# Recurrent scan of a two-layer token mixer: diagonal inverses per segment of four chunks, and log_dt by one contiguous load

## The chip, the cores and the metric

The kernel runs on one core of a Trainium2 chip, in one launch. The metric is the device time of an execution in microseconds (us). A core has five engines that run on their own and meet at semaphores: PE (TensorE, matrix products; its loading of weights is shown as PEld), DVE (VectorE), ACT (ScalarE), POOL (GpSimd) and SP (SyncE, which here only issues DMAs). DMAs are issued by SP, by ACT and by POOL, and sixteen DMA engines carry them out.

## The reference

All data are float32. An input x of 1024 tokens by 1024 features goes through three layers of a network: a gated linear recurrence with a feed-forward part, the "rwkv7" time mix with a feed-forward part, and a hybrid block of a convolution and a diagonal state space (S5). What the change touches lies in two places. The first is the scan of the time mix, for each of 16 heads of 64 features with a state S of 64 x 64:

```
def step(S, inp):
    r_t, w_t, k_t, v_t, a_t, b_t = inp
    sa = einsum('bhvk,bhk->bhv', S, a_t)
    S = S * w_t[:, :, None, :] + sa[..., None] * b_t[:, :, None, :] + v_t[..., None] * k_t[:, :, None, :]
    y = einsum('bhvk,bhk->bhv', S, r_t)
    return S, y
```

The second is the preparation of the S5 part, where each of 32 groups has one value log_dt, and exp(log_dt) multiplies the group's 64 complex rates:

```
dt = exp(log_dt)[:, None]
mag = exp(lr * dt);  ar = mag * cos(li * dt);  ai = mag * sin(li * dt)
```

## The kernel before, in words

Activations lie with the features on the partitions, in tiles of 128 features. The stage that matters here is the time mix. It is one interleaved stage (`weave_`): its parts are written as generators that yield a step (engine, estimated time, what it waits for, what it signals) before the instructions of that step, and a rough clock of the engines decides in which order the steps are issued. The order in each engine's queue is therefore fixed when the program is built, and on the chip each engine works through its queue in that order. The parts are these.

`rwkv_dense` makes the operands of the scan for four segments of 256 tokens. Its `main` runs the projections (L249 to L251 for operands split into a high and a low part, L885 for unsplit ones), `mixes` makes the mixed operands (tiles M and N, `NMP` slots, one mix of 128 features to a slot), `finish` and `stores` put the scan's operands into DRAM, per segment and pair of heads (the last store of a segment is L1038). A mix's slot is free again when the last projection unit that uses it has read it.

`rwkv_scan` works in chunks of 64 tokens, 16 of them, four to a segment, all 16 heads together; two heads (a pair) lie on the partitions. Inside a chunk the recurrence is written with matrices: with A_ab the strictly triangular products of a and b inside the chunk, u = (I - A_ab)^-1 R. For each chunk c:
- `load_bk` loads k and b for half of the pairs (L1114, one slot, `NBK`), `load_q` loads the queries (L1224, slots QT), and `inner` makes the products on PE (L1100) and masks them on DVE into the slot AM of the chunk (L1104). QT and AM have `NAM` slots, so chunk c waits until both halves of chunk c - NAM have been read (signal "y").
- `diagonal` writes the two 32 x 32 diagonal blocks per head of A_ab to DRAM (abD, L1124, four DMAs), and `blocks` loads them back with one block to a partition, four times over: 32 blocks on four groups of 32 partitions (GB, L1133, four DMAs).
- `inverse` starts from rows of the identity (tile `eye`, copied by POOL, L1140) and substitutes: 31 steps s of a product (L1146) and a sum (L1149) on DVE, each over `s // 4 + 1` rows of `31 - s` elements, since each of the four groups of partitions makes every fourth row. Slots GB and YB alternate between two chunks; the last two chunks have slots of their own.
- `inverted` writes the result to DRAM (yiD, L1157, four DMAs that interleave the rows), `whole` loads it into the chunk's matrix YF (L1168, four DMAs), transposes (L1173, DVE) and makes the block below the diagonal with two rounds of small matmuls (L1179, L1189) and ACT copies.
- `turned` brings b, k and v to the tokens' side (L1202 to L1219), `chain` carries the state from chunk to chunk, for two halves of the pairs: R (L1244, L1247, L1250), u (L1255, L1258), then the new state (L1264, L1270, L1274). `outs` makes y (L1289, L1291, L1293), `post` norms and gates it (L1303 to L1324).

`rwkv_out` adds the output projection (mm<-XO, L249 to L251, and HO, L1419) for the first 768 tokens, as soon as the last segment is stored and chunks 7 and 11 are done. After the stage the feed-forward part begins with a norm (sums L273, spread L281, tile ms).

`s5_prep` prepares the S5 part. Its instructions are spread over the feed-forward part that follows, but its first DMAs wait for nothing there: POOL issues them as soon as it has come to them. They are the rates (L1475 to L1477) and log_dt, once as a whole to all partitions (L1479), and twice with every second group, to 64 partitions each (L1481), for 16 columns that hold groups in pairs.

Of the kernel before, what the change touches and what calls it, by code (L numbers as in the profile page):

```python
# [14 lines left out]
P = 128  # L15
# [10 lines left out]
NAM = 3  # L26
# [11 lines left out]
NMP = 13  # L38
# [18 lines left out]
class Net:  # L57
    """Feature-major activations: tile [128 features, 512 tokens] per (k, half)."""
# [15 lines left out]

    def open_group(self, T, W, S, L, psum):
        """Pools of one part of the net: T and S slots of [128, 516], weight slots, PSUM banks per tag."""
        self.close_group()
        self.bigx = ExitStack()
        self.nT = T
        self.big = self.bigx.enter_context(self.tc.tile_pool(name="big", bufs=1, reuse_waits="tile"))  # L80
        self.open_work(W, S, L, psum)

    def open_work(self, W, S, L, psum):
        """All of them but T anew."""
# [8 lines left out]
    def open_top(self):  # L93
        """One more pool above the group's, closed before them."""
        self.close_top()
        self.topx = ExitStack()
        self.top = self.topx.enter_context(self.tc.tile_pool(name="top", bufs=1, reuse_waits="tile"))

    def open_rtop(self):
        """Another one, from the other end of the memory."""  # L100
# [44 lines left out]
    def s(self, dt=F32, n=HT):  # L145
        """scratch [128, n <= 516]"""
# [3 lines left out]
    def extra(self, tag, shape, dt, every, bufs):  # L150
        """now and then a slot of the pool on the right, where that is for more of the others"""
# [7 lines left out]
    def ld(self, src=None, n=HT, rows=P):  # L159
        """tile for a load; loads have slots of their own, for they run ahead"""  # L160
# [66 lines left out]
    def load_ws(self, srcs, nk, m, tag="w"):  # L227
        """srcs: DRAM APs arranged [p, nk, n] for columns c..c+n; returns hi, lo tiles [P, nk, m]"""
# [17 lines left out]
    def mm3(self, ps, w, x, first, last):  # L246
        """ps += w.T @ x with w = (hi, lo), x = (hi, lo)"""
# [5 lines left out]
    # W columns [c0, c0+128) for all nk row tiles  # L253
# [3 lines left out]
    def lin(self, w, xs, nk):  # L257
        """xs: list of (hi, lo) per k -> PSUM tile"""
# [6 lines left out]
    def rstd_bcast(self, acc, scale, eps, acc2=None):  # L265
        """acc [128, 512] -> PSUM [128, 512]: (sum over partitions * scale + eps)^-0.5 on all partitions; with acc2,
        for which that is the factor of another norm: that one and the product of both"""
# [34 lines left out]
    def square(self, h, k, half, gain=None):  # L302
        """h[k][half] is final: its part of the sum of squares (and of that of the products with the gain)"""
# [60 lines left out]
    def blocks(self, nblk, units, in_unit, post, nk_out, wout, h, add_bias=None, lag=2, delay=3, mid=None, late=None, fill=None, nlate=LATE):  # L364
        """units: weight items per block; in_unit(b, i, half, w) ; post(b, half) -> list of nk_out (hi, lo)"""
# [51 lines left out]
        # the first half of the last block before the second half of the one before it  # L417
# [34 lines left out]
    def hawk(self, h, xn, mid, late):  # L452
# [5 lines left out]
        # c8 = 8 softplus(-lam), softplus(z) = max(z, 0) + log1p(exp(-|z|)), log1p(e) = 2 atanh(e / (2 + e))  # L458
# [100 lines left out]
    def ple_prep(self, layer):  # L559
        """p, features on the partitions, split"""  # L560
# [40 lines left out]
    NSEG, SN = 4, 256  # token segments of the dense part  # L601

    def rwkv_consts(self):
# [7 lines left out]
        # block-diagonal ones (2 heads), identity minus the same / 64, and per-head selector columns  # L611
# [8 lines left out]
        # [s, t] masks on both heads: s < t | s <= t  # L620
# [19 lines left out]
        # operands of the scan, one chunk of 64 tokens after another  # L640
        self.qD, self.bkD, self.gbD = (d((16, P, KD, 2, 64), nm) for nm in ("qD", "bkD", "gbD"))
        self.vD = d((16, P, KD, 64), "vD")
        # second factors of the low-rank parts, for one pair after another
# [5 lines left out]
        # per head pair the decays between chunk middles; at the segments' ends in two factors  # L649
# [12 lines left out]
    def rwkv_norm_late(self, hD, rs, half, gain, sig):  # L662
        """A task: the same for the other half, with the factors [tokens, token tiles] known"""
# [22 lines left out]
    def weave_(self, tasks, banks):  # L686
        """Issues the steps of generators in the order in which a rough clock of the engines would start them.
        tasks: (generator, head start in us or a function of PE time and own PE time). banks: PSUM banks per tag.
        A generator yields step(...) before the instructions of that step."""
        clk = {e: 0.0 for e in "PAVGSQD"}  # Q: descriptors, D: transfers  # L690
        free = {tag: [(0.0, f"{tag}{i}") for i in range(n)] for tag, n in banks.items()}
        held, done = {}, {}
        # PE's clock halves after a window of little work, until one of much; windows of several phases
# [70 lines left out]
    def step(eng, us, lat=None, wait=(), sig=(), bank=None, rel=None, par=False, dma=None, use=1.0):  # L764
        """eng: PE, Act, Vector, GpSimd, SP (then us: transfers, lat: their time); us: time on it; lat: after it; wait,
        sig: what it waits for and what is done with it; bank: PSUM tag to take a bank of; rel: bank to give back;
        par: the next step doesn't wait for this one; dma: transfers it starts and their time; use: share of PE's rows and columns."""
# [4 lines left out]
    # r, k, v, the low-rank parts, and from them the operands of the scan (in DRAM)  # L772
# [1513 lines left out]
```

## Time and profile before

| | us |
|---|---|
| median of three runs | 4200.29 |
| lowest and highest | 4192.26, 4203.89 |
| span of the profiled execution, first to last instruction | 4186.6 |
| PE busy in it | 3949.4 |
| DVE busy in it | 2544.7 |
| ACT busy in it | 1466.1 |
| DMA, mean over the span | 111 GB/s |

The profiled execution's own time is not recorded apart from its span; the median lies 13.7 us above the span. In the rows further down a time is counted from the span's start. "Busy" is the time in which an engine has an instruction in work. A matmul's end is modelled, so a busy PE is not a PE at its peak. The clock that PE was granted (PEclk) has two levels, 1.2 and 2.4 GHz; a row gives its mean as a share of 2.4.

### The profile page before, as it was taken

The numbers are of one execution on the slowest core, as the hardware profiler recorded it, in microseconds if no ns is written. First come the engines' busy times: TensorE is split into PE (matmuls) and PEld (weight loads), VectorE is DVE, ScalarE is ACT, GpSimd is POOL, SyncE is SP. The second block draws the span as 40 slices with busy tenths as digits, with TensorE's granted clock in tenths as the row PEclk, the third lists the DMA queues.
The fourth block names the chain that finished last, engine by engine and source line by source line (L and its number), as shares of the span: only waits on it lengthen the run. The fifth ranks groups of instructions, "written<-read, shape, count | busy, mean of one in ns | idle before, by whom it ended". The sixth has DMA issues, their size and how long they took to land.

```text
span 4186.6 us, 58441 instructions
## 1 busy us (share of the span) xinstructions
PE 3949.4 (94%) x22510; PEld 3216.6 (77%) x22510; DVE 2544.7 (61%) x5192; ACT 1466.1 (35%) x2491; POOL 179.3 (4%) x376
## 2 busy tenths in 40 slices
PE   6998999999988999999999699999999999999899
PEld 5776788888877877777867587888887877888687
DVE  6665733333364678777756476354536599997655
ACT  4455511111132665554542241111113332222533
POOL 0000000000000000000000101010100000000000
PEclk8999999999998999989979799999999999999999
DMA  3111111111122789676776541212211244332775
GB/s 103 48 47 34 51 46 51 41 56 51 34 67 88 216 252 237 174 209 170 194 194 173 97 127 52 63 49 66 63 49 58 71 119 118 109 115 96 236 226 186
DMA packets 695830, 464.49 MB, mean 111 GB/s; under 512 B 197956, under 2 KB 620800, under 8 KB 695552
## 3 DMA queue, kind: packets, MB, share of 16 engines
q1 hardware_dynamic: 514272, 367.80, 30.0%
q10 hardware_dynamic: 175872, 83.90, 7.3%
q0 software_dynamic: 5408, 9.06, 1.1%
q8 instruction: 177, 2.90, 0.3%
q14 instruction: 101, 0.83, 0.1%
HBM read 355.51 MB, written 106.69 MB: 110 GB/s over the span
## 4 chain that ended last, share of the span: by engine, by line
PE 69%; DVE 12%; DMA 7%; ACT 5%; issue 4%; SPq 1%; POOL 1%; ACTq 0%; DVEq 0%; POOLq 0%
PE mm L249 15%; PE mm L251 14%; PE mm L250 14%; PE ob L249 4%; PE ob L250 4%; PE ob L251 4%; DVE cy L1882 3%; PE g L1100 2%; PE g L926 1%; PE g L1438 1%; PE y L1291 1%; DMA BK<-bkD 1%; PE y L1289 1%; DVE w L863 1%; PE mm L2073 1%
## 5 line engine op out<-in xcount | busy, mean ns | idle before, releaser
L249 PE MATMUL mm<-T,w 128*128 128x512 f32 (+1 forms) x2944 | 1152.6, 393 | 47.1 <-ACT w L215 22.5
L251 PE MATMUL mm<-T,w 128*128 128x512 f32 (+1 forms) x2944 | 1149.9, 391 | 9.6 <-DVE w L216 9.6
L250 PE MATMUL mm<-T,w 128*128 128x512 f32 (+1 forms) x2944 | 1150.3, 392 | 1.1 <-DVE T L1380 0.9
L249 PEld LDWEIGHTS mm<-T,w 128*128 128x128 f32 x2944 | 558.6, 190 | 174.3 <-ACT w L215 26.9
L251 PEld LDWEIGHTS mm<-T,w 128*128 128x128 f32 x2944 | 559.0, 190 | 126.8 <-DVE w L216 12.1
L250 PEld LDWEIGHTS mm<-T,w 128*128 128x128 f32 x2944 | 559.7, 190 | 117.5 <-DVE T L1380 1.7
L215 ACT CAST w<-wraw 128x1024 fp32r<-128x1024 f32 (+1 forms) x286 | 288.4, 1014 | 988.8 <-PE mm L250 700.2
L216 DVE TENSOR_TENSOR w<-wraw,w 128x1024 fp32r<-128x1024 f32 (+1 forms) x286 | 335.1, 1177 | 373.9 <-ACT w L215 371.1
L389 DVE TENSOR_TENSOR h<-ob,h 128x512 f32<-128x512 f32 x416 | 286.1, 690 | 230.7 <-PE ob L251 227.5
L249 PE MATMUL ob<-S,w 128*128 128x512 f32 x896 | 359.2, 401 | 21.7 <-DVE h L389 21.1
L1882 DVE SCALAR_TENSOR_TENSOR cy<-cu,pv,cy 128x512 f32<-128x512 f32 x480 | 350.9, 749 | 12.3 <-ACT cy L1880 2.6
L250 PE MATMUL ob<-S,w 128*128 128x512 f32 x896 | 354.7, 396 | 0.2 <-DVE S L216 0.2
L251 PE MATMUL ob<-S,w 128*128 128x512 f32 x896 | 354.7, 396 | 0.0
L249 PE MATMUL mm<-M,w 128*128 128x256 f32 x768 | 255.1, 332 | 16.4 <-ACT M L837 8.5
L250 PE MATMUL mm<-N,w 128*128 128x256 f32 x768 | 229.7, 299 | 4.4 <-DVE N L839 4.3
L251 PE MATMUL mm<-M,w 128*128 128x256 f32 x768 | 229.8, 299 | 4.3 <-DVE w L863 4.0
L249 PEld LDWEIGHTS ob<-S,w 128*128 128x128 f32 x896 | 169.9, 190 | 70.2 <-DVE h L389 30.2
L251 PEld LDWEIGHTS ob<-S,w 128*128 128x128 f32 x896 | 169.7, 189 | 38.6
L250 PEld LDWEIGHTS ob<-S,w 128*128 128x128 f32 x896 | 170.1, 190 | 36.3 <-DVE S L216 0.6
L249 PEld LDWEIGHTS mm<-M,w 128*128 128x128 f32 x768 | 157.0, 204 | 50.3 <-issue 23.3
L439 DVE TENSOR_TENSOR S<-mm,S 128x512 f32<-128x512 f32 x88 | 60.8, 690 | 211.7 <-PE mm L251 209.8
L215 ACT CAST S<-S 128x512 fp32r<-128x512 f32 x128 | 79.3, 620 | 266.3 <-DVE S L439 154.4
(458 smaller groups left out, 5431.9 us busy)
## 6 DMA issues: line engine op xcount, KB each, us to landing
wraw<-in_rw_w_rkv_dram ACTq DMA_DIRECT2D x96, 512.0 KB
wraw<-in_ffn_w_in_dram SPq DMA_DIRECT2D x88, 512.0 KB
wraw<-in_w_in_dram SPq DMA_DIRECT2D x48, 512.0 KB
wraw<-in_ffn_w_out_dram SPq DMA_DIRECT2D x44, 512.0 KB
BK<-bkD SPq DMA_DIRECT2D x64, 256.0 KB
wraw<-in_rw_w_o_dram ACTq DMA_DIRECT2D x24, 512.0 KB
wraw<-in_lru_w_in_dram SPq DMA_DIRECT2D x20, 512.0 KB
wraw<-in_ple_w_gate_dram SPq DMA_DIRECT2D x16, 512.0 KB
```

The lines of the kernel that those rows point to most:

```text
L215: self.nc.scalar.copy(hi, x)
L216: self.nc.vector.tensor_sub(lo, x, hi.bitcast(F32))
L249: nc.tensor.matmul(ps, w[0], x[0], start=first, stop=False)
L250: nc.tensor.matmul(ps, w[0], x[1], start=False, stop=False)
L251: nc.tensor.matmul(ps, w[1], x[0], start=False, stop=last)
L389: nc.vector.tensor_add(h[m][half], ps, h[m][half])
L439: nc.vector.tensor_mul(a, ps, sg.pop((b, j, half)))
L863: nc.vector.tensor_sub(wl.rearrange(fl), r.rearrange(fl), wh.bitcast(F32).rearrange(fl))
L926: nc.tensor.matmul(ps, lw[r0:r1, slot, :], HW[hx][r0:r1], start=x == 0, stop=x == len(rows) - 1)
L1100: nc.tensor.matmul(g[:, 128 * x : 128 * x + 128], bk[rs, x].rearrange("p a b -> p (a b)"), qt[rs, j0 + x].rearrange("p a b -> p (a b)"), s ...
L1289: nc.tensor.matmul(o[rs], s[rs, x], qz[rs, j, 1, :], start=True, stop=False)
L1882: nc.vector.scalar_tensor_tensor(y, x[:, k : k + HT], cw(k), y, ALU.mult, ALU.add)
```

## The change

The inverses of the four chunks of a segment are made together. One block lies on one partition: chunk c takes the 32 partitions from 32 * (c % 4), so four chunks fill 128. A step s then covers `s + 1` rows instead of `s // 4 + 1`, and the 31 steps run once per segment. GB and YB have one slot each for all segments (YB 32 x 32 elements instead of 8 x 32), blocks are loaded once instead of four times, and the result is written by one DMA instead of four. The first step waits for the blocks of all four chunks, the loads of a segment's blocks wait for the substitution of the segment before. POOL sets the identity by two memsets. XT and WL share a tile (XW). NAM goes from 3 to 4 and NMP from 13 to 11. In `s5_prep` the two strided loads of log_dt go; two DVE copies take the pairs' columns from the load that stays. The diff also takes out comments and docstrings, which are not shown.

```diff
-NAM = 3
+NAM = 4
-NMP = 13
+NMP = 11
...
-        G, Y = slots("GB", (P, 32, 32), 2, NG), slots("YB", (P, 8, 32), 2, NG)
+        G, Y = (self.tiny(nm, (P, 32, 32), 1) for nm in ("GB", "YB"))
...
-        eye = self.tiny("eye", (P, 8, 32), 1)
-        nc.gpsimd.memset(eye, 0.0)
-        for e in range(4):
-            r = eye[32 * e : 32 * e + 32]
-            nc.gpsimd.affine_select(out=r, in_=r, compare_op=ALU.not_equal, fill=1.0, base=-e,
-                                    pattern=[[-4, 8], [1, 32]], channel_multiplier=0)
...
         def blocks():
             for c in range(NC):
-                yield E("S", 4, 1.46, wait=[("ab", c)] + ([("sub", c - 2)] if 2 <= c < NG else own(c)), sig=[("in", c)], par=True)
-                src = D.pop(c).rearrange("h x j s t -> (h x j) s t")
-                for e in range(4):
-                    nc.sync.dma_start(G(c)[32 * e : 32 * e + 32], src)
-
-        def inverse(q):
-            for c in range(q, NG, 2) if q < 2 else [q]:
-                yield E("G", 0.97, wait=[("in", c)] + ([("yd", c - 2)] if 2 <= c < NG else own(c)))
-                g, y = G(c), Y(c)
-                nc.gpsimd.tensor_copy(y, eye)
+                yield E("S", 1, 0.73, wait=[("ab", c)] + ([("sub", c // per - 1)] if c >= per else []), sig=[("in", c)], par=True)
+                r0 = 32 * (c % per)
+                nc.sync.dma_start(G[r0 : r0 + 32], D.pop(c).rearrange("h x j s t -> (h x j) s t"))
+
+        def inverse():
+            for seg in range(NC // per):
+                yield E("G", 1.2, wait=[("yd", c) for c in range(per * (seg - 1), per * seg)] if seg else ())
+                nc.gpsimd.memset(Y, 0.0)
+                nc.gpsimd.memset(Y.rearrange("p a b -> p (a b)")[:, 0:1024:33], 1.0)
                 for s in range(31):
-                    nj, n = s // 4 + 1, 31 - s
-                    us = 0.07 + nj * n / 960
-                    yield E("V", us, lat=ILAT)
-                    w = self.tiny(f"TB{q % 4}", (P, 80), 2)[:, 0 : nj * n].rearrange("p (j t) -> p j t", t=n)
-                    nc.vector.tensor_mul(w, y[:, 0:nj, s : s + 1].to_broadcast([P, nj, n]),
-                                         g[:, s : s + 1, s + 1 :].to_broadcast([P, nj, n]))
-                    yield E("V", us, lat=ILAT, sig=[("sub", c)] if s == 30 else ())
-                    nc.vector.tensor_add(y[:, 0:nj, s + 1 :], y[:, 0:nj, s + 1 :], w)
+                    nk, n = s + 1, 31 - s
+                    us = 0.07 + nk * n / 960
+                    yield E("V", us, lat=ILAT, wait=() if s else [("in", c) for c in range(per * seg, per * seg + per)])
+                    w = self.tiny("TB", (P, 256), 1)[:, 0 : nk * n].rearrange("p (j t) -> p j t", t=n)
+                    nc.vector.tensor_mul(w, Y[:, 0:nk, s : s + 1].to_broadcast([P, nk, n]),
+                                         G[:, s : s + 1, s + 1 :].to_broadcast([P, nk, n]))
+                    yield E("V", us, lat=ILAT, sig=[("sub", seg)] if s == 30 else ())
+                    nc.vector.tensor_add(Y[:, 0:nk, s + 1 :], Y[:, 0:nk, s + 1 :], w)
 
         def inverted():
             for c in range(NC):
-                yield E("S", 4, 0.73, wait=[("sub", c)], sig=[("yd", c)], par=True)
-                yD = self.dram.tile([2, 2, 8, 32, 32], F32, name=self.n("yiD"))
-                ye = yD.rearrange("h x j (k e) t -> e (h x j) k t", e=4)
-                for e in range(4):
-                    nc.sync.dma_start(ye[e], Y(c)[32 * e : 32 * e + 32])
-                D[c, 1] = yD
+                yield E("S", 1, 0.73, wait=[("sub", c // per)], sig=[("yd", c)], par=True)
+                r0 = 32 * (c % per)
+                D[c, 1] = yD = self.dram.tile([2, 2, 8, 32, 32], F32, name=self.n("yiD"))
+                nc.sync.dma_start(yD.rearrange("h x j k t -> (h x j) k t"), Y[r0 : r0 + 32])
...
-                XT = self.tiny("XT", (P, 8, 32), 1)
+                W = self.tiny("XW", (P, 256), 1)
+                XT = W.rearrange("p (j t) -> p j t", t=32)
...
-                W = self.tiny("WL", (P, 256), 1)
...
-            yield E("S", 9, 1.22, wait=list(wait))
+            yield E("S", 7, 1.22, wait=list(wait))
...
             dma(dt[:, 0:32], ldt.partition_broadcast(P))
-            for b in range(2):
-                dma(dt[64 * b : 64 * b + 64, 32:48], ldt[b:32:2].partition_broadcast(64))
...
+            yield V(16)
+            nc.vector.tensor_copy(dt[lo, 32:48], dt[lo, 0:32:2])
+            yield V(16)
+            nc.vector.tensor_copy(dt[hi, 32:48], dt[hi, 1:32:2])
```

## Rows read from the trace of the kernel before

**Rows 1.** The page's busy line: busy us (share of the span) xinstructions.
```profile
PE 3949.4 (94%) x22510; PEld 3216.6 (77%) x22510; DVE 2544.7 (61%) x5192; ACT 1466.1 (35%) x2491; POOL 179.3 (4%) x376
```

**Rows 2.** Stretches of the scan's stage: length, busy us (xinstructions) by engine, PEclk, DMA, GB/s.
```profile
core 0: us, PE busy (x) PEld busy (x) DVE busy (x) ACT busy (x) POOL busy (x), PEclk, DMA share, GB/s
1560.00:1960.00 400.00, 384.83 (x3922) 315.92 (x3920) 300.39 (x968) 214.78 (x488) 28.41 (x76) 0.93 0.75 199
1960.00:2168.00 208.00, 199.59 (x2208) 158.36 (x2204) 150.04 (x489) 103.73 (x238) 17.80 (x41) 0.90 0.68 180
2168.00:2340.00 172.00, 159.16 (x1644) 128.73 (x1641) 105.31 (x345) 51.70 (x96) 14.34 (x19) 0.89 0.61 176
2340.00:2394.00 54.00, 19.84 (x201) 14.94 (x200) 8.72 (x19) 9.38 (x21) 3.30 (x5) 0.55 0.55 67
```

**Rows 3.** Timeline near 2340: start, us, engine, line, xcount, [idle before, what ended it].
```profile
2338.20 1.66 POOL L1481 DMA_DIRECT2D pv<-in_ssm_log_dt_dram  x2
2340.65 21.20 SPq L1157 DMA_DIRECT2D yiD<-YB  x4
2366.76 0.44 DVE L1173 STREAM_TRANSPOSE XT<-YF 32x256 f32<-32x256 f32 x1 [14.36 <-DMA YF<-yiD]
2367.25 0.31 PE L1179 MATMUL g<-XT,AM 32*32 32x32 f32 x2 [26.58 <-DVE XT L1173]
```

**Rows 4.** DMA view of 2338 to 2363: a queue's packets and share; issues, landing us.
```profile
q0 software_dynamic: 136, 0.03, 71.3%
pv<-in_ssm_log_dt_dram POOLq DMA_DIRECT2D x2, 4.0 KB, 18.0
```

**Rows 5.** Timeline near 2285, where chunk 14 goes the same way.
```profile
2282.16 2.52 SPq L1157 DMA_DIRECT2D yiD<-YB  x4
2286.18 1.81 SPq L1168 DMA_DIRECT2D YF<-yiD  x4
2289.93 0.90 DVE L1173 STREAM_TRANSPOSE XT<-YF 32x256 f32<-32x256 f32 x2
```

**Rows 6.** A small DVE copy in the S5 preparation: duration in ns, minimum, median, maximum.
```profile
L1486 DVE COPY pv<-ms x1: 198/198/198, 2461.0 to 2461.0; 128x48 f32<-128x48 f32 x1
```

**Rows 7.** Groups from 1100 to 2600 us, DVE: busy us, mean ns, idle before.
```profile
L1146 DVE TENSOR_TENSOR TB<-YB,GB 128x60 f32<-128x60 f32 (+24 forms) x496 | 99.0, 208 | 19.2 <-DMA GB<-abD 9.3 <-POOL YB L1140 1.8 <-DMA L<-rkD 0.4
L1149 DVE TENSOR_TENSOR YB<-YB,TB 128x60 f32<-128x60 f32 (+24 forms) x496 | 98.0, 207 | 7.4
L1013 DVE TENSOR_TENSOR L<-L,F 128x256 f32<-128x256 f32 x32 | 13.3, 417 | 2.8 <-ACT F L1009 2.8
```

**Rows 8.** The same view, PE: first matmuls on split mixed operands.
```profile
L249 PE MATMUL mm<-M,w 128*128 128x256 f32 x768 | 255.1, 332 | 16.4 <-ACT M L837 8.5 <-ACT w L861 7.7
```

**Rows 9.** SP's timeline, 2164 to 2290 us: a store, two loads, a write.
```profile
2165.25 0.37 SPq L1038 DMA_DIRECT2D gbD<-GBs  x1
2187.17 0.32 SPq L1114 DMA_DIRECT2D BK<-bkD  x1
...
2232.73 2.55 SPq L1157 DMA_DIRECT2D yiD<-YB  x4
2235.66 0.33 SPq L1114 DMA_DIRECT2D BK<-bkD  x1
```

**Rows 10.** DVE's timeline: inverse of chunk 12; last mask and inverse of chunk 15.
```profile
2205.83 0.19 DVE L1146 TENSOR_TENSOR TB<-YB,GB 128x31 f32<-128x31 f32 x1 [1.22 <-DMA GB<-abD]
...
2302.94 0.69 DVE L1104 TENSOR_TENSOR AM<-g,msk 128x512 f32<-128x512 f32 x1 [5.76 <-PE g L1100]
...
2312.78 0.18 DVE L1146 TENSOR_TENSOR TB<-YB,GB 128x31 f32<-128x31 f32 x1
```

**Rows 11.** PE's timeline: u of chunks 13, 14 and 15; next stage's spread.
```profile
2284.48 1.98 PE L1255 MATMUL ch<-R,YF 64*64 64x64 f32 x32
...
2308.33 1.15 PE L1255 MATMUL ch<-R,YF 64*64 64x64 f32 x32
...
2372.04 1.97 PE L1255 MATMUL ch<-R,YF 64*64 64x64 f32 x32 [0.88 <-ACT YF L1194]
...
2393.76 0.58 PE L281 MATMUL ms<-ident,rs 128*128 128x128 f32 x1 [1.73 <-POOL rs L290]
```

More of the change, by code (lines that the diff above doesn't have):

```diff
@@ L1119, in diagonal @@
                 yield E("S", 4, 0.73, wait=[("am", c)], sig=[("ab", c)], par=True)
-                abD = self.dram.tile([2, 2, 8, 32, 32], F32, name=self.n("abD"))
+                D[c] = abD = self.dram.tile([2, 2, 8, 32, 32], F32, name=self.n("abD"))
                 for hd in range(2):
@@ L1125, in diagonal @@
                                           AM(c)[r0 : r0 + 32, :, hd, 0, 32 * x : 32 * x + 32])
-                D[c] = abD
         def blocks():
             for c in range(NC):
-                yield E("S", 4, 1.46, wait=[("ab", c)] + ([("sub", c - 2)] if 2 <= c < NG else own(c)), sig=[("in", c)], par=True)
-                src = D.pop(c).rearrange("h x j s t -> (h x j) s t")
-                for e in range(4):
-                    nc.sync.dma_start(G(c)[32 * e : 32 * e + 32], src)
-        def inverse(q):
-            for c in range(q, NG, 2) if q < 2 else [q]:
-                yield E("G", 0.97, wait=[("in", c)] + ([("yd", c - 2)] if 2 <= c < NG else own(c)))
-                g, y = G(c), Y(c)
-                nc.gpsimd.tensor_copy(y, eye)
-                for s in range(31):
-                    nj, n = s // 4 + 1, 31 - s
-                    us = 0.07 + nj * n / 960
-                    yield E("V", us, lat=ILAT)
-                    w = self.tiny(f"TB{q % 4}", (P, 80), 2)[:, 0 : nj * n].rearrange("p (j t) -> p j t", t=n)
-                    nc.vector.tensor_mul(w, y[:, 0:nj, s : s + 1].to_broadcast([P, nj, n]),
-                                         g[:, s : s + 1, s + 1 :].to_broadcast([P, nj, n]))
-                    yield E("V", us, lat=ILAT, sig=[("sub", c)] if s == 30 else ())
-                    nc.vector.tensor_add(y[:, 0:nj, s + 1 :], y[:, 0:nj, s + 1 :], w)
@@ L1330, in outputs @@
                 nc.sync.dma_start(self.outD[:, :, 64 * c : 64 * c + 64].rearrange("j p t -> p j t"), O[c % 2])
-        return ([chain(0), chain(1), outs(0), outs(1), whole(), [inverse(q) for q in [0, 1, *range(NG, NC)]], blocks(), turned(), [inner(), load_bk()], diagonal(),
+        return ([chain(0), chain(1), outs(0), outs(1), whole(), inverse(), blocks(), turned(), [inner(), load_bk()], diagonal(),
                  inverted(), load_q(), post(), outputs()])
```

## The prediction

> **What bounds the kernel now.** I read the page's busy line first [rows 1]: PE is busy 3949.4 of 4186.6 us, DVE 2544.7. As a whole the kernel hangs on PE, so an edit that removes DVE work pays only where PE waits. The profiled execution has a span of 4186.6 us; the median of the three runs is 4200.29, so some 13.7 us lie around the span if that execution was a median one (the fastest, 4192.26, leaves 5.7). I work with differences and put them on the median.
>
> The second view is the table by stretches of the stage that the change touches, the recurrent mixer, from 1560 us, when its scan begins, to 2394 [rows 2]. Up to 2168 us PE is busy about 96% of the time at 0.90 to 0.93 of its clock. Until 2340 us it is still 159.16 of 172. In the last stretch, 54 us long, it works 19.84 us at 0.55 of the clock. So there is slack in one place only: the end of the scan, where chunk 15 (the last of 64 tokens) is finished while nothing else is left.
>
> The third view is the timeline of those 54 us [rows 3]. POOL issues the two strided log_dt loads of the next stage's preparation at 2338.20. SP begins to write chunk 15's inverses (yiD<-YB) at 2340.65, and these four issues take 21.20 us. The transpose of the blocks, loaded back from there, follows at 2366.76, and PE resumes at 2367.25 after 26.58 us idle, the longest gap of the stage. The DMA view of 2338 to 2363 names who was in the way [rows 4]: POOL's queue q0 moved 0.03 MB in 136 packets and held 71.3% of sixteen engines' time; the two log_dt loads, 4 KB each, took 18.0 us in the median to land.
>
> **log_dt.** The change drops both strided loads; the contiguous one was there already. What the write costs without them I take from chunk 14 [rows 5]: issue at 2282.16, all four in 2.52 us, next load at 2286.18, transpose at 2289.93, so 7.77 us from write to transpose. For chunk 15 it is 2366.76 - 2340.65 = 26.11. The term is 26.11 - 7.77 = 18.3 us, taken from the path that sets the end, as PE has no other work there. Bounds: 0 if something else held the write; 18.3, not 26.58, as the normal 7.8 us stay. In return DVE copies 64 x 16 elements twice; a copy of 128 x 48 takes 198 ns [rows 6], so under 0.4 us, on a DVE that was busy 8.72 of 54 us [rows 2]. Uncovered, ACT's exponential comes 0.4 us later.
>
> The Trainium skill (DMA: Bandwidth & Descriptors, "Queues, rings and completion order") says that each DMA engine takes turns between the queue rows that have work, packet by packet. Read as a fair share, SP's writes would have lost only half their rate, the term would be about 9 us and the forecast 4191. The row speaks for nearly the whole.
>
> **The inverse on DVE.** Before, each chunk has 31 steps of a product and a sum, 62 operations x 16 chunks = 992, on average (1560 elements over 31 steps) 50 elements per partition, at 208 and 207 ns [rows 7]: 992 x 0.2075 = 206 us. After, 62 x 4 segments = 248 operations, (s+1)(31-s) elements, 5456 over 31 steps, 176 on average. 256 elements take 417 ns [rows 7]; the line through both is 1.02 ns an element, so 176 take 0.335 us and the sum is 83 us. DVE loses 123 us and 744 instructions, but up to 2168 us that lies beside a PE that is 96% busy [rows 2], and PE's waits for DVE are small. SP issues 10 instead of 16 DMAs a chunk (96 fewer, at 0.63 us as in the write's 2.52 for four [rows 5], 60 us of queue time). I credit both with 8 us of PE waits, between 0 and the 24 us that PE idles from 1560 to 2168 (608 - 584.42) [rows 2]. POOL's two memsets a segment replace four copies and run while the blocks are still on their way; XT and WL become one tile, but WL was written after XT had been read before too; TB's one buffer is written and read on DVE alone: all three nothing, at worst a wait of one operation, 0.3 us.
>
> **Slots.** NAM 3 to 4 gives each chunk of a segment its own products (AM) and queries. It is paid with two of 13 slots for mixed operands (NMP 11). PE's first matmuls on those operands waited 16.4 us in all, 8.5 of it for ACT's cast [rows 8]. With 11 slots five mixes instead of three are made during a last unit; I take 4 us more, between 0 and 20 (as much again, and some). Earlier segments cost nothing else: their scan has the next segment's projections beside it; without that cover each waits one inverse, some 30 us.
>
> **The end of the scan, rebuilt.** Here the change adds a wait: the inverse of chunk 12 now waits for the blocks of chunk 15. Behind it on DVE stand the transposes and state updates of chunks 12 to 15, and for those PE and ACT wait.
> 1. The last segment is stored at 2165.25; the half-chunk loads of the products (BK, one slot) go from 2187.17 to 2235.66 in five steps [rows 9], 9.7 us each. Without the slot wait the eighth goes at 2245.4, and the last mask of chunk 15 comes one step later, 2255, instead of 2302.94 [rows 10], where chunk 15 waited until chunk 12 had given its slot back. The first of these steps also waited for chunk 11's remainder, which will be done earlier: I take 2250 (2232 to 2258).
> 2. Mask to first operation of the inverse: 2302.94 to 2312.78 [rows 10], 9.8 us: 2260.
> 3. The inverse: 62 x 0.335 = 20.8 us plus other DVE work in between. For chunk 12 the wall time was 2205.83 to 2232.73 [rows 9, 10], 26.9 for 12.9 of its own, 14 of other work; I take 10: 2291 (21 to 35 us).
> 4. Write, load, transpose: 7.8 as above: 2299.
> 5. Transpose to u of chunk 12: as for chunk 15, 2366.76 to 2372.04 [rows 3, 11], 5.3: 2304.
> 6. Three more chunks. Bounds: chunk 15 alone kept PE 19.84 us at 0.55 of the clock [rows 2], 11 us at full clock; chunk 13's u to chunk 14's was 23.85 us with projections in between [rows 11]; R2 below has 30. I take 19 each: 2361.
> 7. u of the last chunk to the next stage's first spread (ms): 2372.04 to 2393.76, 21.7 [rows 11], at half the clock; I take 20: 2381.
> Against 2393.76 that is -13. So the tail gains less than the 18.3 of log_dt: the batch itself costs 5 there. With -8 for waits and +4 for slots the sum is -17, rounded to -18: **4182**.
>
> **Rivals.**
> R1, given back: steps 1 and 3 at their late ends (+8, +4) and the slots at +10 turn the sum of -17 into about +1: 4200. For it: PE had only 13 us of gaps from 2168 to 2340 [rows 2], so chunk-by-chunk inverses were well covered. Against it: the slot wait of chunk 15 goes.
> R2, slower: the chain at half clock. The projection matmuls (mm<-XO) that now lie between the chunks can run while the batch waits for its blocks. If they are used up before step 5, PE pauses, its clock falls to 1.2 GHz as in the last 54 us [rows 2], and four chunks of small matmuls run at it: chunk 15's 19.84 us, some 4 more for the update of the state and the turned operands that chunk 15 has behind it or doesn't need, and with gaps 30 instead of 19: +33 in step 6, +2 in step 7, 4217. It decides from the point where those matmuls run out 10 us or more before the first u. For it: chunk 15 alone ran so. Against it: while they last the clock is full, 0.89 on average to 2340.
> The Trainium skill (TensorE: Matmul & The Clock Gate, Part 1) says that PE's clock follows how busy PE has lately been, and that idle time halves it; by that rule every pause that the batch makes costs twice, which is R2's price. The trace agrees at 2340 to 2394.
> R3, more: step 1 at its early end (-18) and step 6 at 14 each (-15), as PE has less beside the chunks than in the 23.85 us; two thirds of both is 22 us, 4160. For it: the slot wait and the POOL and SP work of the last chunk of the third segment are gone. Against it: one BK slot, so the pace of 9.7 us stays.
> R4, the log_dt edit does not do what it says, or by half: if the write was held by turns and not wholly, 9 us come back instead of 18.3, 4191, and if other traffic held it, none, 4200.
>
> **Numbers.** Forecast 4182 (own range 4168 to 4190), chance 0.36. R3 0.14, R1 0.25, R2 0.21, R4 0.04. What a measurement can tell from no change is 0.3%, 12.6 us. Faster by more: 0.33 of the forecast's 0.36 plus R3's 0.14, 0.47. Same: 0.03 + R1's 0.25 + R4's 0.04 less 0.01 at R1's upper end, 0.31. Slower: 0.21 + 0.01, 0.22. The range runs from just below R3 to just above R2, 4150 to 4220.
>
> **What would show it.** No gap of over 12 us on PE in front of the last transposes, and yiD's issue at about 0.6 us: log_dt right. 124 products of the inverse in place of 496, at 0.33 us mean: the inverse right. First operation of the last inverse near 2260 and its last near 2291 after the span's start: steps 1 to 3. The u of chunks 12 to 15 some 19 us apart, at full clock: step 6; some 30 apart at 0.5 of the clock would be R2. Waits of PE for the mixes (L249) far above 20 us would make the slots' term wrong. The forecast falls if chunk 12's u comes after 2325, or if the stage before 2165 moves by more than 10 us.

## The result and the profile after

The change made the kernel slower: 4215.6 us in the median of six runs against 4197.8 us of the kernel before, ratio 1.0054 (95% interval 1.0034 to 1.0074), some 18 to 23 us. The forecast was 4182 us. The profiled execution of after has a span of 4218.3 us and took 4219.97 us, the longest of its six; that of before has 4186.6 us, and since some 2 us lie around the span in other runs of before, it was about 9 us faster than the median. So 14 of the 31.7 us between the two spans are scatter, and sizes are taken below from the timed runs, places from the traces.

The page's busy line after, against [rows 1]: PE works 24 us longer, VectorE 84 us less with 742 instructions fewer (the durations of its instructions, added up, fall by 122; where two overlap, the busy time counts them once).

```profile
PE 3973.7 (94%) x22510; PEld 3228.4 (77%) x22510; DVE 2460.5 (58%) x4450; ACT 1468.5 (35%) x2491; POOL 177.3 (4%) x361
```

At 1340 us the two traces are level within 0.4 us, and of the 32.6 us by which the last matmul is later, 30.9 have arrived at the first spread of the next stage. So the time went in the mixer's stage. In it PE is busy 979.0 us (1340 to 2425) where it was 960.5 (1340 to 2394), for the same 9241 matmuls, and idle 106 us instead of 94. Its stretches after, with the columns of [rows 2]:

```profile
core 0: us, PE busy (x) PEld busy (x) DVE busy (x) ACT busy (x) POOL busy (x), PEclk, DMA share, GB/s
1560.00:1960.00 400.00, 381.73 (x3589) 309.51 (x3585) 266.92 (x612) 216.91 (x491) 30.55 (x72) 0.94 0.70 191
1960.00:2100.00 140.00, 133.94 (x1507) 111.66 (x1503) 87.77 (x191) 69.57 (x150) 8.89 (x22) 0.98 0.67 184
2100.00:2160.00 60.00, 56.26 (x482) 38.74 (x482) 26.19 (x68) 23.93 (x60) 4.13 (x16) 0.50 0.48 120
2160.00:2340.00 180.00, 157.58 (x1478) 126.77 (x1476) 84.39 (x170) 49.88 (x93) 5.88 (x5) 0.84 0.55 164
2340.00:2425.00 85.00, 60.14 (x1013) 48.91 (x1008) 23.04 (x49) 29.57 (x65) 11.56 (x15) 0.81 0.41 118
```

The third row stands out. From 2100 to 2160 us PE runs at half its clock and does 482 matmuls; the same window before, in the first row below, has 601 at 0.84. The last projection starts at 2092 us after and at 2137 before: after, the projections have run ahead of the scan, and what is left is the scan's own matmuls, most of 64 columns, and the last operands of the fourth segment.

```profile
2100.00:2160.00 60.00, 57.19 (x601) 41.56 (x602) 42.00 (x141) 28.84 (x72) 5.79 (x18) 0.84 0.63 159
2140.00:2160.00 20.00, 18.34 (x130) 11.72 (x132) 12.72 (x35) 9.41 (x26) 1.29 (x7) 0.52 0.61 138
2160.00:2180.00 20.00, 17.09 (x169) 12.12 (x166) 6.67 (x16) 6.05 (x13) 0.00 (x0) 0.55 0.84 245
```

But before has such a stretch too, behind its own last projection: the second and third row, which the stretches of [rows 2] hide. And the kernel of experiment 6 below, which is faster than after, has one as early:

```profile
2100.00:2120.00 20.00, 14.96 (x48) 8.17 (x50) 16.18 (x51) 7.80 (x21) 2.20 (x9) 0.50 0.58 142
2120.00:2140.00 20.00, 14.19 (x216) 11.04 (x215) 11.29 (x30) 6.88 (x16) 0.15 (x1) 0.59 0.73 186
```

So the half clock alone does not tell after from before. What does is the time from the last projection to the last store of the segment: 90 us after (2092 to 2181), 28 before (2137 to 2165), 50 in experiment 6 (2083 to 2132). Here the projections' first matmuls on split operands, before and then after, from the view of their tile; the last two times of a row are the first and the last start:

```profile
L249 PE MATMUL mm<-M,w x768: 277/285/687, 1352.3 to 2137.0; 128*128 128x256 f32 x192
L249 PE MATMUL mm<-M,w x768: 276/285/775, 1348.8 to 2091.6; 128*128 128x256 f32 x192
```

The end of the scan after, from the timeline: last store of the last segment, first and last operation of the last inverse, the write, the transposes, u of chunk 12, the last spread.

```profile
2181.39 0.46 SPq L1038 DMA_DIRECT2D gbD<-GBs  x1
...
2282.76 0.19 DVE L1138 TENSOR_TENSOR TB<-YB,GB 128x31 f32<-128x31 f32 x1 [0.82 <-DMA GB<-abD]
...
2315.43 0.22 DVE L1141 TENSOR_TENSOR YB<-YB,TB 128x31 f32<-128x31 f32 x1
...
2319.07 1.87 SPq L1148 DMA_DIRECT2D yiD<-YB  x4
...
2326.34 0.90 DVE L1165 STREAM_TRANSPOSE XW<-YF 32x256 f32<-32x256 f32 x2 [3.93 <-DMA YF<-yiD]
...
2336.25 1.15 PE L1246 MATMUL ch<-R,YF 64*64 64x64 f32 x32
...
2424.66 2.08 PE L281 MATMUL ms<-ident,rs 128*128 128x128 f32 x8 [1.34 <-POOL rs L290]
```

The write takes 1.87 us for four chunks where that of chunk 15 alone took 21.20 [rows 3], and the transpose follows 7.3 us behind it. But the segment is stored 16 us later than before [rows 9] (the third one at 1938 us in both), the u of chunk 12 comes at 2336, and the spread 31 us later than in [rows 11].

### The profile page after: what moved, and what is told of

It is laid out like the page before. It is cut to its first block, busy times and chain, and to the rows that moved or that the text cites. A ratio compares the mean times of both kernels' runs of the same rounds, so it can differ in the third digit from the quotient of the medians.

```text
span 4218.3 us, 57574 instructions
## 1 busy us (share of the span) xinstructions
PE 3973.7 (94%) x22510; PEld 3228.4 (77%) x22510; DVE 2460.5 (58%) x4450; ACT 1468.5 (35%) x2491; POOL 177.3 (4%) x361
## 4 chain that ended last, share of the span: by engine, by line
PE 68%; DVE 13%; DMA 7%; issue 6%; ACT 4%; POOL 1%; SPq 0%; ACTq 0%; DVEq 0%; POOLq 0%
PE mm L249 14%; PE mm L251 14%; PE mm L250 14%; PE ob L249 4%; PE ob L250 4%; PE ob L251 4%; DVE cy L1875 3%; PE g L1094 2%; PE g L926 2%; PE mm L885 1%; DVE w L863 1%; DMA BK<-bkD 1%; DVE w L216 1%; PE g L1429 1%; PE y L1282 1%
## 5 line engine op out<-in xcount | busy, mean ns | idle before, releaser
L249 PE MATMUL mm<-M,w 128*128 128x256 f32 x768 | 252.8, 329 | 18.4 <-ACT M L837 11.1
```

The lines of the kernel that those rows point to most:

```text
L249: nc.tensor.matmul(ps, w[0], x[0], start=first, stop=False)
```

## The experiments

Each was timed against the kernel before; the ratio is to that, with its 95% interval. There were three series (1 to 4, 5 to 8, 9 to 11), in which the kernel before had medians of 4197.1, 4195.7 and 4204.6 us; from one series to another the ratios compare better than the medians.

**1. log_dt alone**

```diff
 (the kernel before)
-            for b in range(2):
-                dma(dt[64 * b : 64 * b + 64, 32:48], ldt[b:32:2].partition_broadcast(64))
...
+            nc.vector.tensor_copy(dt[lo, 32:48], dt[lo, 0:32:2])
+            nc.vector.tensor_copy(dt[hi, 32:48], dt[hi, 1:32:2])
```

> The kernel before with the log_dt edit alone (two strided loads gone, two copies on VectorE in their place); all else as before. My term: the write of chunk 15's inverses is no longer held by POOL's strided loads, write to transpose goes from 26.1 to about 8 us, and 18 us come off the end of the scan: 4180 us against 4198, ratio 0.9956, and the 26.6 us gap on PE becomes about 8. Rival (something else held that write): no change, 4198, with the gap still there. Half (the queues shared the engines): 4189.

Measured: 4175.0 us, 0.9951 (0.9933 to 0.9968), 21 us less. In the timeline the write of chunk 15 goes straight through, its transpose comes 6.6 us later, and PE's gap of 26.58 us [rows 3] is 7.11. The profiled execution is the slowest of the eight, and this write comes 16 us later in it than in [rows 3]:

```profile
2356.55 2.69 SPq L1157 DMA_DIRECT2D yiD<-YB  x4
...
2363.14 0.44 DVE L1173 STREAM_TRANSPOSE XT<-YF 32x256 f32<-32x256 f32 x1 [5.07 <-DMA YF<-yiD]
...
2363.64 0.31 PE L1179 MATMUL g<-XT,AM 32*32 32x32 f32 x2 [7.11 <-DVE XT L1173]
```

**2. The batch with the strided loads put back**

```diff
 (the kernel after)
+            for b in range(2):
+                dma(dt[64 * b : 64 * b + 64, 32:48], ldt[b:32:2].partition_broadcast(64))
-            nc.vector.tensor_copy(dt[lo, 32:48], dt[lo, 0:32:2])
-            nc.vector.tensor_copy(dt[hi, 32:48], dt[hi, 1:32:2])
```

> The kernel after with the two strided log_dt loads of before put back: the batched inverse alone. In the trace of after POOL issues its contiguous log_dt load at 2392.2 us, just ahead of the store of chunk 14's outputs (2397.7 us), and chunk 15's group norm waits for that store. If strided loads hold whatever SP writes next for some 18 us, that store lands about 15 to 18 us later and the kernel takes 4231 to 4234 us. Rival (nothing on the path is issued behind them now, or the loads' price was peculiar to the write of the inverses): 4216, as after.

Measured: 4234.5 us, 1.0102 (1.0074 to 1.0129), 19 to 20 us above after. So log_dt is worth the same in both kernels, though here it holds up other work. ACT's exponential, which stands in front of chunk 15's squares, waits for the loads, and the store of chunk 14, for which the squares wait too, lands 21 us after its issue instead of 4. The squares start at 2420.11 instead of 2402.08, in an execution that was 1.9 us behind by then:

```profile
2417.78 0.24 ACT L1480 ACTIVATE pv<-pv 128x48 f32<-128x48 f32 x1 [19.91 <-DMA pv<-in_ssm_log_dt_dram]
2420.11 0.60 ACT L1297 ACTIVATE psq<-g 128x512 f32<-128x512 f32 x1 [2.09 <-DMA outD<-psq]
```

**3. Eleven slots alone**

```diff
 (the kernel of experiment 1)
-NMP = 13
+NMP = 11
```

> The kernel before with the log_dt edit and 11 instead of 13 slots for mixed operands (NMP); the inverse still chunk by chunk, three slots of products. Theory S, the slots: in the trace of after the last segment is stored 16.5 us later than before (2181.9 against 2165.3), and two slots fewer alone do that; then this kernel takes about 16 us more than the log_dt edit alone, near 4196 us. Theory B, the batch: the scan falls behind because four chunks wait for one inverse; then this kernel is within 4 us of the log_dt edit alone, near 4180 us, and its last store stays near 2165.

Measured: 4238.8 us, 1.0109 (1.0087 to 1.0132): 64 us above the log_dt edit alone, four times what theory S said. The whole stage, first with 13 slots (experiment 1), then with 11:

```profile
1340.00:2389.00 1049.00, 963.11 (x9243) 788.57 (x9244) 712.41 (x2120) 524.92 (x1155) 73.11 (x176) 0.90 0.71 192
```

```profile
1340.00:2436.00 1096.00, 987.57 (x9234) 802.69 (x9235) 713.83 (x2119) 526.93 (x1154) 78.85 (x176) 0.88 0.68 183
```

That is 47 of the 64 us, in the slowest execution of the one kernel and one of the faster of the other. The same matmuls take 24 us more at a lower clock, and PE idles 108 us instead of 86. The projections come later (below in the same view, first with 13 slots, then with 11: the last starts at 2185 instead of 2149) and part of the scan earlier: the u of chunk 7, the last of the second segment, starts at 1930 us instead of 1978.

```profile
L249 PE MATMUL mm<-M,w x768: 277/285/775, 1350.9 to 2148.5; 128*128 128x256 f32 x192
L249 PE MATMUL mm<-M,w x768: 277/285/775, 1346.7 to 2185.4; 128*128 128x256 f32 x192
```

In SP's timeline with 11 slots the last store of the third segment goes at 1997 us (with 13 at 1936), that of the fourth at 2214 (2176):

```profile
1995.64 1.62 SPq L1038 DMA_DIRECT2D gbD<-GBs  x2
...
2214.31 0.37 SPq L1038 DMA_DIRECT2D gbD<-GBs  x1
```

The waits of PE's first matmuls for the mixes show nothing of it; from 1100 to 2600 us they are 15.6 us, against 16.4 in [rows 8] (those of the other three lines of the projections add up to 20 us, against 12 with 13 slots):

```profile
L249 PE MATMUL mm<-M,w 128*128 128x256 f32 x768 | 258.6, 337 | 15.6 <-ACT M L837 10.3 <-ACT w L861 4.9
```

**4. The tile of the group norm elsewhere in memory**

```diff
 (the kernel after)
-        YF = slots("YF", (P, 8, 64), 2, NG, True)
+        self.tiny("psq", (P, HT), 1); YF = slots("YF", (P, 8, 64), 2, NG, True)
```

> The kernel after, with one slot of memory moved: the 2048 bytes of the group norm's squares and outputs (psq) come first in the scan's memory instead of behind the states. In the trace of after the first activation of the next stage's norm (L309) starts at 2413.8 us, behind the store of chunk 15's outputs, because its tile lies on psq's place; before it ran at 2370. Theory O, the overlay: without that wait it follows chunk 15's activations at 2403.2, and about 10.6 us come off: 4205 us, ratio to before 1.003. Rival (the order of ACT, or PE and VectorE that have to finish chunk 15 anyway, sets the start): 4214 to 4216, as after.

Measured: 4226.9 us, 1.0069 (1.0046 to 1.0093); its median is 11 us above after and the intervals overlap, so no gain can be told. The wait is gone as meant, but the gap on PE that it was held responsible for shrinks by 3 us only. Here the timeline at the end of the stage, of after first, then of this kernel:

```profile
2413.81 0.63 ACT L309 ACTIVATE L<-h 128x512 f32<-128x512 f32 x1 [10.65 <-DMA outD<-psq]
...
2421.45 1.86 PE L273 MATMUL ms<-ones,L 128*128 128x1 f32 x8 [12.80 <-DVE L L313]
```

```profile
2419.66 0.64 ACT L309 ACTIVATE L<-h 128x512 f32<-128x512 f32 x1
...
2426.84 0.69 DVE L1315 TENSOR_TENSOR psq<-PY,gb 128x512 f32<-128x512 f32 x1
2427.45 4.66 DVE L313 TENSOR_TENSOR L<-L,S 128x512 f32<-128x512 f32 x6
...
2435.01 1.86 PE L273 MATMUL ms<-ones,L 128*128 128x1 f32 x8 [9.73 <-DVE L L313]
```

The sums of the next norm (L313) stand behind chunk 15's group norm in VectorE's order. Before, ACT's part of them ran at 2370.07, ahead of it (timeline of before):

```profile
2370.07 0.63 ACT L309 ACTIVATE L<-h 128x512 f32<-128x512 f32 x1
```

**5. Twelve slots, chunk by chunk**

```diff
 (the kernel of experiment 1)
-NMP = 13
+NMP = 12
```

> The kernel before with the log_dt edit and 12 slots for mixed operands, one fewer than before; the inverse chunk by chunk. With 13 slots the log_dt edit alone took 4175 us, with 11 it took 4239. Theory S1 (each slot is worth about the same): half of the 64 us, near 4207 us. Theory S2 (a step: 12 slots still give the projections the operands of the next unit in time, 11 don't): at most 4182 us.

Measured: 4184.9 us, 0.9993 (0.9966 to 1.0019); its runs lie between 4173 and 4223, further apart than those of any other kernel here. The first slot costs 10 us by the medians (18 by the ratios), the second 54 (49): neither theory quite, nearer the step.

**6. The batch with twelve slots**

```diff
 (the kernel after)
-NMP = 11
+NMP = 12
...
-                vt = self.tiny("V", (P, 8, 64), 1)
+                vt = self.tiny("BK2", (P, 8, 64), 1)
```

> The kernel after with 12 instead of 11 slots for mixed operands; their 2048 bytes come from letting the loads of v and of b, k in the turned operands share one buffer. The batch of four chunks stays. Theory S, the slots are what made after slow: the last segment's store comes back from 2182 to 2170 us or earlier, and the time falls by 20 to 35 us, to 4181 to 4196 us. Theory B, the batch itself (its wait for four chunks) made it slow: 4210 to 4220 us, as after; the shared buffer can only cost.

Measured: 4191.7 us, 0.9988 (0.9974 to 1.0001), 24 us below after, with the batch untouched. Theory S holds: one slot is worth that much here. In SP's timeline the last segment is stored at 2132 us, not 2181:

```profile
2132.34 0.38 SPq L1038 DMA_DIRECT2D gbD<-GBs  x1
```

**7. Two chunks together, eleven slots**

```diff
 (the kernel after)
-            for seg in range(NC // per):
+            for q in range(NC // 2):
+                rs = slice(64 * (q % 2), 64 * (q % 2) + 64)
...
-                    yield E("V", us, lat=ILAT, wait=() if s else [("in", c) for c in range(per * seg, per * seg + per)])
+                    yield E("V", us, lat=ILAT, wait=() if s else [("in", c) for c in (2 * q, 2 * q + 1)])
```

> The kernel after with the diagonal inverses made for two chunks together instead of four, on 64 partitions, the two halves of the tiles by turns; 496 operations of VectorE instead of 248, 11 slots as in after. Theory B, four chunks waiting for one inverse let the scan fall behind: its first chunks get their u some 20 us earlier in each segment, and the time falls by 15 to 25 us, to 4191 to 4200 us. Theory S, the slots set the pace: within 8 us of after, 4208 to 4224 us.

Measured: 4209.8 us, 1.0040 (1.0022 to 1.0059), 6 us below after, within what theory S allowed, and the intervals overlap: with 11 slots it changes little how many chunks wait for an inverse.

**8. Two chunks together, twelve slots** (the diffs of 6 and 7)

> Both: inverses for two chunks together and 12 slots (with the shared load buffer). If the slots and the size of the batch each cost what the theories S and B say, the two gains add up to 35 to 60 us and the time is 4156 to 4181 us, level with the log_dt edit alone (4175 us) or better. If only the slots count, as the kernel with four chunks and 12 slots, 4181 to 4196 us; if only the batch counts, as pairs with 11 slots.

Measured: 4172.7 us, 0.9942 (0.9920 to 0.9964). It beats both kernels, and is level with the log_dt edit alone. With 12 slots the size of the batch does count: pairs are 19 us below fours (experiment 6), and the intervals are apart. Slot and pairs win 24 and 6 us one by one and 43 together, so they do not simply add up. The gap in front of the next norm is there in this kernel too, so a better order has still something to win. PE's timeline:

```profile
2377.10 1.86 PE L273 MATMUL ms<-ones,L 128*128 128x1 f32 x8 [12.87 <-DVE L L313]
```

**9. The order for eleven slots, with thirteen in memory**

```diff
 (the kernel of experiment 3)
-                hi, lo = (rtop(f"{y}{m % mpairs}", (P, n), 1, F32R) for y in "MN")
+                hi, lo = (rtop(f"{y}{m % 13}", (P, n), 1, F32R) for y in "MN")
```

> The kernel before with the log_dt edit and an order of work written as for 11 slots, but with 13 slots in memory (the planner's waits count 11, the tiles 13). It tells the slots themselves from the order that the planner writes for them. Theory P, the order: instructions stand in every engine's queue as in the kernel with 11 slots, and that order costs the 64 us whether memory is there or not: 4225 to 4245 us. Theory W, the wait for a free slot: with 13 in memory the waits are gone, and it comes back to the log_dt edit alone, 4170 to 4185 us. Half and half would be near 4205.

Measured: 4256.2 us, 1.0113 (1.0085 to 1.0142), as experiment 3 by the ratio; the median lies 11 us above the range of theory P, in a series in which before is 7 us higher too. In the traces the two kernels have the same instructions in the same order on VectorE and ACT, and on PE but for two matmuls. In this kernel, then, it is the order that costs, not a wait for memory: the two slots that it has in hand give nothing back.

**10. Pairs, slots dealt out as 12 and 10**

```diff
 (the kernel of experiment 7)
-                hi, lo = (rtop(f"{y}{m % mpairs}", (P, n), 1, F32R) for y in "MN")
+                hi, lo = rtop(f"M{m % mpairs}", (P, n), 1, F32R), rtop(f"N{z % 10}", (P, n), 1, F32R)
```

> Inverses for two chunks together, and the same memory as the kernel after, but dealt out otherwise: 12 slots for the high parts of mixed operands (and the exact ones) and 10 for the low parts, which only the split operands need, instead of 11 and 11; v keeps its own buffer. Theory S, the slots set the pace and 12 suffice: as pairs with 12 slots, 4165 to 4185 us, below the log_dt edit alone or level with it. If the low parts are what ran short, 4205 to 4215 us, as pairs with 11 slots.

Measured: 4186.0 us, 0.9961 (0.9940 to 0.9981), a little over the expected 4165 to 4185 and far from 4205: with no byte more than after, 30 us below it by the medians, 39 by the ratios. Against experiment 7, from which it differs in the slots alone, it is 24 and 33 us.

**11. Chunk by chunk, slots as 14 and 12** (the same edit on the kernel of experiment 1, with 14 and 12)

> The kernel before with the log_dt edit and its 26 places for mixed operands dealt out as 14 for the high parts and 12 for the low instead of 13 and 13; inverse chunk by chunk. If more room ahead still speeds the projections (13 to 11 cost 64 us), it is 5 to 15 us below the log_dt edit alone: 4160 to 4170 us. If 13 are enough, level: 4172 to 4180 us. If the low parts bind at 12, as 12 slots of both: 4180 to 4190 us.

Measured: 4184.3 us, 0.9958 (0.9939 to 0.9978). By its ratio it is level with the log_dt edit alone; the median of before was 7 us higher in that series. So more than thirteen high slots win nothing. Its median lies in the range named for the case that the low parts bind at 12, and a price of a few us for them is not excluded.

## Why the prediction was wrong

**The step that failed is the slots**: "I take 4 us more, between 0 and 20". It is the term of the sum that was mis-sized: 13 to 11 slots measured 64 us by itself (experiment 3), and in the kernel with the batch one slot alone is worth 24 us (experiment 6), with pairs 37 (experiments 7 and 8). I priced a shortage as waits of PE at its matmuls, by [rows 8], and named those waits as the sign that would refute me. They stayed at 15.6 us in experiment 3 and 18.4 in after. What was missed is that the order of every queue is written out ahead by `weave_`, so a slot that is not free yet becomes another order, not a wait for it. In experiment 3 that order has the projections later and part of the scan earlier, and experiment 9 shows that it costs as much with the memory there. About half of what the traces of 3 and 1 differ by is PE's work at a lower clock, which is busy time and no wait at all; the other half is idle time, spread over many lines.

In after, with the batch, the order is another one: the projections end 45 us earlier than before, and the last segment is stored 16 us later all the same. PE's order shows why: from the last projection to that store it has 816 matmuls in after, most of them the scan's of chunks 8 to 10, done at 0.60 of the clock between those that make the segment's operands, against some 200 in before and 225 in experiment 6. One slot more brings the store from 2181 to 2132 us (experiment 6). Why the planner's order changes so much with one slot stays open. The two stretches, after first, then experiment 6:

```profile
2092.00:2181.00 89.00, 81.23 (x816) 55.72 (x816) 38.26 (x100) 36.91 (x94) 4.78 (x20) 0.60 0.47 117
```

```profile
2083.00:2132.00 49.00, 36.80 (x225) 21.56 (x226) 41.04 (x117) 19.69 (x51) 3.89 (x17) 0.55 0.60 145
```

**log_dt** was right: 18.3 us forecast, 21 measured alone, and some 16 for chunk 15's squares in experiment 2. The Trainium skill (DMA: Bandwidth & Descriptors, "Queues, rings and completion order") has the engines take turns between queue rows, packet by packet; read as a fair share of the time that made 9 us, and the measurement decides against that reading, though not against the turns (see the last section).

**The inverse on VectorE** was right in its own size: 124 products at 339 ns forecast 335, 83.9 us in all where 83 were forecast. The groups of VectorE after, with the columns of [rows 7]:

```profile
L1138 DVE TENSOR_TENSOR TB<-YB,GB 128x31 f32<-128x31 f32 (+15 forms) x124 | 42.0, 339 | 4.6 <-DMA GB<-abD 2.2
L1141 DVE TENSOR_TENSOR YB<-YB,TB 128x31 f32<-128x31 f32 (+15 forms) x124 | 41.9, 338 | 2.1
```

What the batch is worth to the kernel was not a number of its own. I had it at -3 us (8 off for waits, 5 more in the tail). With 11 slots it takes back 23 us (4215.6 against 4238.8), with 12 nothing that can be told (4191.7 against 4184.9). The steps -21, +64 and -23 lead from before to after, and their +20 is no confirmation: the -23 is what is left over. It also holds the fourth slot of products (NAM), which was never run by itself, and with pairs and 12 slots the batch is no more than level with the log_dt edit alone.

**The tail**, step by step, in the trace of after, where the last spread was forecast at 2381 and came at 2425. Step 1, last mask of chunk 15: 2250 forecast, 2271 measured; 16 of the 21 us are the late store of the segment, which I had taken as unmoved and named as a reason for the forecast to fall. Step 2: 11.5 us, forecast 9.8. Step 3: 32.9 us, forecast 31. Step 4: 10.7 from the last sum to the transpose, forecast 7.8. Step 5: 9.9, forecast 5.3. Step 6: the last u at 2383.9, so 47.6 us for three chunks, forecast 57, at 0.98 and 0.93 of the clock from 2340 to 2380. Step 7: 40.8, forecast 20. Its 20.8 us too much, the second large miss, are two orders that I had not looked at. VectorE's copies of log_dt stand between two steps of chunk 14's group norm and wait for the load; chunk 15's squares wait for chunk 14's store. And the sums of the next norm, which ran beside chunk 15 before, come behind it. In front of that norm PE waited at most 1.4 us in the kernel before and in experiments 1, 3, 5 and 9, and 8.0 in 11, all chunk by chunk; in after and experiments 2, 6, 7, 8 and 10, with batches, 12.8 to 13.3. So that part comes with the batch and not with the slots, and the forecast had nothing for it. What puts it there was not settled: moving the tile took 3 us of it (experiment 4). The timeline of after shows the load, the copy that stands 2.03 us for it, and chunk 15's squares 5.97 us late behind the store:

```profile
2392.21 0.57 POOL L1470 DMA_DIRECT2D pv<-in_ssm_log_dt_dram  x1
...
2395.48 0.17 DVE L1478 COPY pv<-pv 64x16 f32<-64x16 f32 x1 [2.03 <-DMA pv<-in_ssm_log_dt_dram]
...
2402.08 0.60 ACT L1297 ACTIVATE psq<-g 128x512 f32<-128x512 f32 x1 [5.97 <-DMA outD<-psq]
```

**The rivals.** R2 had the measured time (4217) by the wrong way: the four chunks of the tail ran 16 us apart at nearly full clock, not 30 at half of it. The half clock came some 200 us earlier, while the last segment's operands were still being made, where R2 did not look; the kernel before has a stretch of it there too. R1's remedy, slots at +10, was too small by far; R3 and R4 did not happen.

## What to carry to other kernels

Where a planner writes the order of every queue, memory that is taken from one part need not be paid in waits for that memory: price it by the order that comes out, and time that edit alone before it is hidden in a larger one. A change that pays with another part's slots should be run in three pieces, what it wins, what it pays, and both; here the payment (64 us) was nearly three times what the batch won back (23), and one slot given back made up for the loss. Compare two kernels at the same point of the work, not at the same microsecond: the half clock at 2100 looked new and had only come earlier. A short transfer issued beside a chain is priced by what is queued with it, not by its bytes.

## What the runs showed of the hardware

Two strided loads of 4 KB each kept SP's next transfer back for about 17 to 18 us in both cases seen: in [rows 3] the write of the inverses, in experiment 2 the store of chunk 14. The queue of POOL moved 0.01 MB in 61 packets from 2398 to 2420 us there and held 71.3% of the engines' time, as in [rows 4]; the row is from its DMA view.

```profile
q0 software_dynamic: 61, 0.01, 71.3%
```

The packets in the traces tell why bytes say so little. In before the two loads are 32 packets of 256 bytes that take 7.7 to 9.0 us each, in two rounds that begin near 2342 and 2352 us; the 16 packets of 1 KB of the contiguous load take 0.2 to 0.8 us. Between the rounds, from 2348 to 2352, SP's queue starts 144 packets, and none from 2342 to 2348 nor from 2352 to 2359. So there a turn was taken, but each round cost some 8 us. In experiment 2 (6.4 to 9.4 us a packet) SP's queue got none between the rounds.

PE's clock stood at 0.50, its level of 1.2 GHz, for 60 us from 2100 on in after, while the trace calls PE 94% busy; before that, until 2092, projections of 256 columns ran beside the scan at 0.98. The same instructions in the same order met the clock differently in another execution: the kernel of experiment 4 has the order of after, and from 1620 to 1640 us the clock was 0.95 in after and 0.50 there, with PE busy all the time in both. The two rows of the stretches, after first:

```profile
1620.00:1640.00 20.00, 20.00 (x138) 16.51 (x138) 14.70 (x33) 9.68 (x21) 1.15 (x5) 0.95 0.60 154
```

```profile
1620.00:1640.00 20.00, 20.00 (x71) 14.61 (x70) 5.41 (x12) 6.70 (x17) 1.03 (x4) 0.50 0.40 100
```

The Trainium skill (TensorE: Matmul & The Clock Gate, Part 1) lets the clock follow how busy PE has been. By the trace PE was equally busy in both windows; a matmul's end is modelled in it, so it cannot refute the page either. At 1620 us the execution of experiment 4 was 5 us behind the other, at the matmul that after starts at 1640 it was 13 behind, and it stayed 10 to 18 us behind to the end of the scan; runs of the kernel before lie up to 0.8% apart (4177.8 to 4212.0 us), so sizes had to come from several of them.
